# Decay chain and dt-scaled inputs in PSUM banks: a one-layer hybrid attention and state-space kernel

## The chip, the core and the metric

The kernel runs on one core of a Trainium2 chip. The metric is the device time of one execution in microseconds (us). Engines are named as in the profile: PE (TensorE matmul), PEld (its weight load), DVE (VectorE), ACT (ScalarE), POOL (GpSimd) and SP (the queue that issues the loads).

## What is computed

One layer: a projection of the normed input feeds sparse attention and a Mamba-2 state-space mixer; both are merged, and a gated MLP follows. The change lies in the mixer, which works on 4 chunks of 128 tokens and 4 groups of 8 heads:

```python
x = (xh.astype(f32) * dt[..., None]).reshape(b, nc, q, g, r, p)
a_cum = jnp.cumsum(adt, axis=2)
seg = a_cum[:, :, :, None] - a_cum[:, :, None, :]
decay = jnp.exp(jnp.where(tri[None, None, :, :, None, None], seg, -jnp.inf))
cb = jnp.einsum("bclgn,bcsgn->bclsg", cm, bm)
y_diag = jnp.einsum("bclsgr,bcsgrp->bclgrp", cb[..., None] * decay, x)
states = jnp.einsum("bclgn,bclgrp->bcgrpn", bm, x * decay_states[..., None])
```

## The kernel before

All matrices are split into a high and a low part in the matmul format (`hi` on ACT, `lo = src - hi` on DVE or, for weights, on POOL), and three matmuls make one product. Weights come through `weight()`: a 512 KB load on SP, `wh` on ACT (L86), `wl` on POOL (L87).

The mixer runs group by group. `ssd_chain` writes the steps of one group; `weave` spreads matmul work that does not depend on them between the steps: the projections `pxbc` of the next group (convolved on DVE, L388), the gate projections `pz`, and the output projection `pso` of the group before. The top-128 search of the indexer (L332, L333, tile `msk`) is independent DVE work beside groups 0 and 1. A scheduler of the framework then fixes each engine's order and the buffers of each pool, and every engine executes its own order strictly.

Two steps matter here. `prep_M` builds the masked decay matrix of four heads: a load of the cumulative sums as `dec` (128x512), four subtractions (L524), an exponential on ACT (L526), the product with `cb` (L527), and the split into `Mh` (ACT) and `Ml` (DVE). `prep_x` transposes a chunk into the PSUM tile `px`, scales it by dt into the SBUF tile `xdt` (L500), makes `y` (L502), splits `xdt` into `X2` (printed as X) in two halves (L507 ACT, L508 DVE), scales `xdt` once more in place (L513) and splits it into `xwh` and `xwl`. `diag` multiplies `M` by `X2` into `py`. There are 32 `prep_M` and 16 `prep_x`; 12 of these make `xw`.

PSUM has two pools of four banks: `pm` (through `mmt`) for the long projections, `pc` (through `cht`) for everything small: `pcb`, `px`, `py`, `po`, `pst`, `pB`, `pyT`.

Of the kernel before, what the change touches and what calls it, by code (L numbers as in the profile page):

```python
# [9 lines left out]
F32 = mybir.dt.float32  # L10
# [4 lines left out]
P = 128  # L15
# [7 lines left out]
HG = 8  # L23
# [25 lines left out]
def _body(ctx, tc, x, prm_d, cst_d, nfin_d, wI_d, wX_d, wSO_d, wQ_d, wG_d, wAO_d, wO_d, wUp_d, wDn_d,  # L49
# [32 lines left out]
    ident = cv("ident")  # L82

    def split(hi, lo, src, lo_eng=None):
        """hi = fp32r(src), lo = fp32r(src - hi)."""
        nc.scalar.activation(hi, src, AF.Copy)  # L86
        (lo_eng or nc.vector).tensor_tensor(lo, src, f(hi), OP.subtract)  # L87

# [10 lines left out]
        return hi, lo  # L99

    def mm3(ps, terms):
        """ps = sum of lhs.T @ rhs over terms of ((lhs_hi, lhs_lo), (rhs_hi, rhs_lo))."""
        seq = [(a[0], b[0]) for a, b in terms] + [(a[0], b[1]) for a, b in terms] + [(a[1], b[0]) for a, b in terms]
        for i, (l, r) in enumerate(seq):
            nc.tensor.matmul(ps, l, r, start=(i == 0), stop=(i == len(seq) - 1))  # L105

    def rsqrt(dst, ss, scale, eps, n, pool):
        """dst = (ss*scale + eps)^-0.5"""
        t = pool.tile([P, n], F32, tag="rsq", name="rsq")
        nc.vector.tensor_scalar(t, ss, scale, eps, OP.mult, OP.add)  # L110
        nc.gpsimd.tensor_tensor(dst, t, mhalf[:, :n], OP.pow)
# [5 lines left out]
            for k in range(KD)]  # L117

    def norm_T(xts, gname, dst, pool, sq, scl):
        """dst = rmsnorm(xts).T in hi and lo; sq and scl: the engine (ACT or DVE) of each block's squares and scaling."""  # L120
        for hf in range(2):
            alloc = mmt if hf == 0 else cht
            ps = [alloc(f"nT{gname}{hf}{i}").rearrange("p (k n) -> p k n", k=2) for i in range(KD // 2)]
            for bb in range(2):
                b = 2 * hf + bb
                xn = pool.tile([P, D], F32, tag="xn", name=f"xn{gname}{b}", bufs=4)
                ss = pool.tile([P, 1], F32, tag="nss", name=f"nss{gname}{b}", bufs=4)
                rs = pool.tile([P, 1], F32, tag="nrs", name=f"nrs{gname}{b}", bufs=4)
                if sq[b] == "v":
                    nc.vector.scalar_tensor_tensor(xn, xts[b], 1.0, xts[b], OP.mult, OP.mult, accum_out=ss)  # L130
                else:
                    nc.scalar.activation(xn, xts[b], AF.Square, accum_out=ss)
                rsqrt(rs, ss, 1.0 / D, EPS, 1, pool)
                if scl[b] == "a":
                    nc.scalar.activation(xn, xts[b], AF.Copy, scale=rs)
                else:
                    nc.vector.tensor_scalar(xn, xts[b], rs, None, OP.mult)
                for k in range(KD):
                    nc.tensor.transpose(ps[k // 2][:, k % 2, bb * P:(bb + 1) * P], xn[:, k * P:(k + 1) * P], ident)
            hs = slice(hf * 256, (hf + 1) * 256)  # L140
            for k in range(KD):
                g = pv(gname, k, k + 1)
                p_ = ps[k // 2][:, k % 2, :]
                nc.scalar.activation(dst[k][0][:, hs], p_, AF.Copy, scale=g)  # L144
                nc.vector.scalar_tensor_tensor(dst[k][1][:, hs], p_, g, f(dst[k][0][:, hs]), OP.mult, OP.subtract)
# [6 lines left out]
    def proj_T(ps, w):  # L152
        mm3(ps, [((w[0][:, k * P:(k + 1) * P], w[1][:, k * P:(k + 1) * P]), actT[k]) for k in range(KD)])

# [1 line left out]
    mid_stack = ExitStack()  # L156
    mid = mid_stack.enter_context(tc.tile_pool(name="mid", bufs=1, side="right"))
    ckvT = (mid.tile([P, S], R32, tag="ckh", name="ckh"), mid.tile([P, S], R32, tag="ckl", name="ckl"))
# [16 lines left out]
    with tc.tile_pool(name="n1", bufs=2) as n1:  # L175
# [15 lines left out]
        nc.sync.dma_start(cs1, cst_d[:, NKEEP:])  # L191
        norm_T(xts, "gmix", actT, n1, "vava", "aavv")

# [1 line left out]
        ps = mmt("pkidx")  # L195
        psc = mmt("pcr")
        for hf in range(2):
# [33 lines left out]
            nc.scalar.activation(ckvT[0], pk, AF.Copy)  # L231
            nc.vector.tensor_tensor(ckvT[1], pk, f(ckvT[0]), OP.subtract)

# [1 line left out]
        dx = dtS.rearrange("p a b -> p (a b)")  # L235
        e = n1.tile([P, 128], F32, tag="sp_e", name="sp_e", bufs=1)
        z = n1.tile([P, 128], F32, tag="sp_z", name="sp_z", bufs=1)
# [35 lines left out]

        latent()

# [1 line left out]
        pu = cht("pu")  # L277
        nc.tensor.matmul(pu[:H, :UW], pv("relb")[:BUCKETS, :], oh, start=True, stop=True)
        us = n1.tile([H, UW], F32, tag="us", name="us", bufs=1)
        nc.vector.tensor_copy(us, pu[:H, :UW])  # L280
        nc.sync.dma_start(uD, us)

# [1 line left out]
    nc.vector.tensor_copy(msk[:, 0:P], cv("maskc"))  # L284
    sds = ExitStack()
    sd = sds.enter_context(tc.tile_pool(name="sd", bufs=2))

    def dup_q(ps, name, tags, pool, scale, bufs):
        """Per head of a pair, its rows hi and lo on both halves of the partitions."""
        out = []  # L290
        for hh in range(2):
            r, o = slice(64 * hh, 64 * hh + 64), slice(64 - 64 * hh, 128 - 64 * hh)
            hi = pool.tile([P, S], R32, tag=tags[2 * hh], name=f"{name}h{hh}", bufs=bufs)
            lo = pool.tile([P, S], R32, tag=tags[2 * hh + 1], name=f"{name}l{hh}", bufs=bufs)
            nc.scalar.activation(hi[r], ps[r], AF.Copy, scale=scale)
            nc.vector.scalar_tensor_tensor(lo[r], ps[r], scale, f(hi[r]), OP.mult, OP.subtract)
            nc.sync.dma_start(f(hi[o]), f(hi[r]))
            nc.sync.dma_start(f(lo[o]), f(lo[r]))
            out.append((hi, lo))
        return out  # L300
# [37 lines left out]
            out += [lambda r=rnd, k=k: r(k=k) for k in range(16)]  # L338
        return out

# [1 line left out]
    def weave(chain, fill):  # L342
        """Emit the chain's (weight, step)s in order, the fillers spread between them by weight."""
        total = sum(w for w, _ in chain) or 1
        acc = done = 0
        for w, step in chain:
            step()
            acc += w
            want = int(len(fill) * acc / total + 1e-6)
            for k in range(done, want):  # L350
                fill[k]()
            done = want
        for k in range(done, len(fill)):
            fill[k]()

    def proj_steps(name, wsrc, after, parts=2):
        """One column tile of a projection of actT, in emission steps."""
        st = {}

        def seq():  # L360
# [114 lines left out]
    def ssd_chain(g, X, Z, uss):  # L475
# [17 lines left out]
        def prep_x(c):  # L493
# [2 lines left out]
            for j in range(4):  # L496
                nc.tensor.transpose(px[:, j * P:(j + 1) * P], X[j][:, cs], ident)
            px3 = px.rearrange("p (r q) -> p r q", r=HG)
            xdt = sd.tile([P, HG, 64], F32, tag="xdt", name=f"xdt{g}_{c}", bufs=1)
            nc.vector.tensor_tensor(xdt, px3, bc(dtS[:, c, hs], 64), OP.mult)  # L500
            y = sd.tile([P, HG, 64], F32, tag="y", name=f"y{g}_{c}", bufs=4)
            nc.vector.tensor_tensor(y, px3, bc(pv("dsk")[:, hs], 64), OP.mult)  # L502
            st["y"][c] = y
            for half in range(2):
                X2 = sd.tile([P, 4, 2, 64], R32, tag="X2", name=f"X2{g}_{c}_{half}", bufs=4)
                xh = xdt[:, 4 * half:4 * half + 4, :]
                nc.scalar.activation(X2[:, :, 0, :], xh, AF.Copy)  # L507
                nc.vector.tensor_tensor(X2[:, :, 1, :], xh, f(X2[:, :, 0, :]), OP.subtract)  # L508
                st["X2"][c, half] = X2
            if c < NB - 1:  # L510
                xwh = sd.tile([P, S], R32, tag="xwh", name=f"xwh{g}_{c}", bufs=1)
                xwl = sd.tile([P, S], R32, tag="xwl", name=f"xwl{g}_{c}", bufs=1)
                nc.vector.tensor_tensor(xdt, xdt, bc(dst8[:, c, hs], 64), OP.mult)  # L513
                split(xwh, xwl, xdt.rearrange("p r q -> p (r q)"), lo_eng=nc.vector)
                st["xw"][c] = (xwh, xwl)

        def prep_M(c, half):
# [2 lines left out]
            nc.sync.dma_start(dec, bass.AP(tensor=acD.tensor, offset=acD.offset + (c * 32 + r0) * P,  # L520
                                           ap=[[0, P], [1, 4 * P]]))
            cbb = st["cb"][:, c, :].unsqueeze(1).to_broadcast([P, 4, P])
            for r in range(4):
                nc.vector.tensor_scalar(dec[:, r, :], dec[:, r, :], acS[:, c, r0 + r:r0 + r + 1], 0.0,  # L524
                                        OP.subtract, OP.min)
            nc.scalar.activation(dec, dec, AF.Exp)  # L526
            nc.vector.tensor_tensor(dec, dec, cbb, OP.mult)  # L527
            Mh = sd.tile([P, 4, P], R32, tag="Mh", name=f"Mh{g}_{c}_{half}", bufs=3)
            Ml = sd.tile([P, 4, P], R32, tag="Ml", name=f"Ml{g}_{c}_{half}", bufs=3)
            split(Mh, Ml, dec, lo_eng=nc.vector)  # L530
            st["M"][c, half] = (Mh, Ml)

        def diag(c, half):
# [114 lines left out]
    prev[0]()  # L648
    last_trans, so_last = prev[1:]

# [1 line left out]
    attT = []  # L652
    ao_stack = ExitStack()

# [128 lines left out]
    crs = {}  # L783

    def pav_(h):
        """Even heads: [Vh|Vl], odd heads: [Vl|Vh], so that the low part lands on the other half of the partitions."""
        p, hh = h // 2, h % 2
        r, o_ = slice(64 * hh, 64 * hh + 64), slice(64 - 64 * hh, 128 - 64 * hh)
        V, PT = Vs[p // 2], PTs[h]
# [65 lines left out]
        weave(chain, fl)  # L855
    att_split(7)

# [1 line left out]
    at.close()  # L859
    nxs = ExitStack()  # L860
    nx = nxs.enter_context(tc.tile_pool(name="nx", bufs=1, side="right"))
# [15 lines left out]
        split(hi, lo, tg)  # L877
        mg.append((hi, lo))

# [1 line left out]
    x1 = [big.tile([P, D], F32, tag=f"ys{b}", name=f"x1{b}") for b in range(NB)]  # L881
    for b in range(NB):
        nc.sync.dma_start(x1[b], x[b * P:(b + 1) * P, :])
# [120 lines left out]


def _coltile(w):
    """(K, N) -> (N/128, 128, K/128 * 128): per column tile, rows on partitions."""
    k, n = w.shape
    return np.ascontiguousarray(w.reshape(k // P, P, n // P, P).transpose(2, 1, 0, 3)).reshape(n // P, P, k)

# [75 lines left out]
```

## Time and profile before

| | us |
|---|---|
| three runs | 1187.9, 1189.9, 1190.06; median 1189.9 |
| span of the profiled execution | 1188.0 |
| PE busy | 1113.1 (94%) |
| DVE busy | 705.9 (59%) |
| ACT busy | 582.3 (49%) |
| POOL busy | 518.0 (44%) |

The profiled execution is known by its span alone; the median of the runs is 1.9 us above it. An instruction counts as busy from its start to its end, also where it has started and is held up, so a DVE instruction that is far longer than others of its form has been waiting inside its own bar. The mixer takes from about 76 us to 480 us, attention to about 690, merge and output projection to 820, the MLP the rest.

### The profile page before, as it was taken

The page shows a single profiled execution, that of the slowest core. Times are in us where ns is not written, and L with a number is a line of the kernel's source. Part 1 is how long each engine was busy: PE and PEld are TensorE (multiplying, and loading weights), DVE is VectorE, ACT ScalarE, POOL GpSimd, SP SyncE. Part 2 cuts the span into 40 slices and gives each one's busy share as a digit, 9 for nine tenths or more (in the row PEclk, how much of TensorE's full clock was granted, in tenths as well). Part 3 has the DMA queues.
Part 4 walks back from the last instruction along what each step waited for, and adds up shares of the span by engine and source line. Part 5 has one row for each costly group of instructions (what it writes and reads, how often), then busy time and mean ns, then how long its engine had stood idle before and what let it go on. Part 6 is the DMA issues. An engine that isn't in the chain of part 4 may idle for free.

```text
span 1188.0 us, 14616 instructions
## 1 busy us (share of the span) xinstructions
PE 1113.1 (94%) x5268; PEld 920.8 (78%) x5268; DVE 705.9 (59%) x1324; ACT 582.3 (49%) x942; POOL 518.0 (44%) x287
## 2 busy tenths in 40 slices
PE   5898996998999889899999899999999999999997
PEld 5677775876887678778878788888888888888885
DVE  5569999998579689368988833305533344330004
ACT  5356464557476555456667633215444444432113
POOL 3324343334524434566566444444444444444442
PEclk9989999999999899999999999999999999999999
DMA  5264322222322231443434133232332222222221
GB/s 186 90 184 143 107 81 80 89 87 74 116 80 83 86 116 59 122 127 107 129 102 125 47 110 123 107 110 86 106 106 90 104 91 99 97 89 107 89 105 73
DMA packets 43306, 122.06 MB, mean 103 GB/s; under 512 B 5393, under 2 KB 9761, under 8 KB 43233
## 3 DMA queue, kind: packets, MB, share of 16 engines
q1 hardware_dynamic: 42656, 120.07, 30.5%
q8 instruction: 42, 0.69, 0.2%
q10 hardware_dynamic: 576, 1.05, 0.2%
q14 instruction: 32, 0.25, 0.1%
HBM read 108.29 MB, written 5.32 MB: 96 GB/s over the span
## 4 chain that ended last, share of the span: by engine, by line
PE 57%; DVE 26%; ACT 5%; issue 3%; POOL 2%; DMA 2%; POOLq 0%; DVEq 0%; ACTq 0%
PE pup L105 20%; PE pdn L947 10%; PE pso L464 5%; PE pao L105 4%; PE pga L105 4%; PE pwo L891 3%; DVE dec L524 3%; DVE u L388 3%; PE pxbc L373 3%; DVE msk L333 2%; DVE dec L527 2%; DVE m L332 2%; DVE pr L747 1%; DVE pr L759 1%; DVE Ml L87 1%
## 5 line engine op out<-in xcount | busy, mean ns | idle before, releaser
L87 POOL TENSOR_TENSOR wl<-wr,wh 128x1024 fp32r<-128x1024 f32 x168 | 409.8, 2440 | 481.4 <-ACT wh L86 260.6
L86 ACT ACTIVATE wh<-wr 128x1024 fp32r<-128x1024 f32 x168 | 177.4, 1057 | 189.1 <-PE pdn L947 80.6
L930 DVE SCALAR_TENSOR_TENSOR fu<-pup,prm,fu 128x511 f32<-128x511 f32 x88 | 65.9, 749 | 124.2 <-ACT fu L928 122.6
L105 PE MATMUL pup<-hTh,wh 128*128 128x512 f32 (+1 forms) x368 | 88.0, 381 | 1.6 <-ACT hTh L144 0.8
L105 PE MATMUL pup<-hTl,wh 128*128 128x512 f32 (+1 forms) x368 | 87.7, 380 | 0.0
L105 PE MATMUL pup<-hTh,wl 128*128 128x512 f32 (+1 forms) x368 | 87.5, 380 | 0.0
L105 PEld LDWEIGHTS pup<-hTh,wh 128*128 128x128 f32 x368 | 67.2, 188 | 15.1 <-ACT hTh L144 1.1
L105 PEld LDWEIGHTS pup<-hTl,wh 128*128 128x128 f32 x368 | 67.2, 188 | 13.1
L105 PEld LDWEIGHTS pup<-hTh,wl 128*128 128x128 f32 x368 | 67.2, 188 | 13.1
L947 PE MATMUL pdn<-wl,fh 128*128 128x512 f32 x176 | 68.6, 390 | 1.2 <-POOL wl L87 1.2
L947 PE MATMUL pdn<-wh,fl 128*128 128x512 f32 x176 | 68.5, 389 | 0.0
L947 PE MATMUL pdn<-wh,fh 128*128 128x512 f32 x176 | 68.4, 390 | 0.0
L974 DVE TENSOR_TENSOR x<-pdn,x 128x512 f32<-128x512 f32 x8 | 5.5, 690 | 104.6 <-PE pdn L947 104.6
L439 PE MATMUL pz<-wh,hTh 128*128 128x512 f32 x128 | 52.4, 409 | 9.9 <-DVE u L388 9.9
L388 DVE SCALAR_TENSOR_TENSOR u<-pxbc,prm,u 128x511 f32<-128x511 f32 (+2 forms) x72 | 53.2, 739 | 9.7 <-ACT u L386 9.3
L373 PE MATMUL pxbc<-hTh,wh 128*128 128x512 f32 x192 | 53.8, 413 | 4.1 <-ACT wh L86 2.9
L524 DVE TENSOR_SCALAR dec<-dec,acS 128x128 f32<-128x128 f32 x128 | 50.6, 450 | 8.9 <-DMA dec<-acD 8.9
L373 PE MATMUL pxbc<-hTh,wl 128*128 128x512 f32 x192 | 51.1, 393 | 0.0
L440 PE MATMUL pz<-wl,hTh 128*128 128x512 f32 x128 | 50.9, 398 | 0.0
L441 PE MATMUL pz<-wh,hTl 128*128 128x512 f32 x128 | 50.9, 398 | 0.0
L373 PE MATMUL pxbc<-hTl,wh 128*128 128x512 f32 x192 | 50.0, 391 | 0.0
L464 PE MATMUL pso<-yTh,wh 128*128 128x512 f32 x128 | 38.7, 426 | 11.4 <-ACT wh L86 7.9
(360 smaller groups left out, 2554.2 us busy)
## 6 DMA issues: line engine op xcount, KB each, us to landing
wr<-wUp SPq DMA_DIRECT2D x44, 512.0 KB, 3.4
wr<-wX SPq DMA_DIRECT2D x40, 512.0 KB, 3.5
wr<-wDn SPq DMA_DIRECT2D x22, 512.0 KB, 3.5
dec<-acD SPq DMA_DIRECT2D x32, 256.0 KB, 3.3
wr<-wSO SPq DMA_DIRECT2D x16, 512.0 KB, 3.5
wr<-wG SPq DMA_DIRECT2D x16, 512.0 KB, 3.6
x<-x SPq DMA_DIRECT2D x8, 512.0 KB, 4.9
wr<-wQ SPq DMA_DIRECT2D x8, 512.0 KB, 3.5
```

Source lines behind the costliest of these rows:

```text
L86: nc.scalar.activation(hi, src, AF.Copy)
L87: (lo_eng or nc.vector).tensor_tensor(lo, src, f(hi), OP.subtract)
L105: nc.tensor.matmul(ps, l, r, start=(i == 0), stop=(i == len(seq) - 1))
L373: nc.tensor.matmul(st["ps"], *st["it"][i], start=(i == 0), stop=(i == 23))
L388: nc.vector.scalar_tensor_tensor(u[:, d:], ps[:, :S - d], pv("cw", o + 3 - d, o + 4 - d), u[:, d:], OP.mult, OP.add)
L439: nc.tensor.matmul(ps, actT[k][0][:, bs], wh[:, ws], start=(k == 0), stop=False)
L440: nc.tensor.matmul(ps, actT[k][0][:, bs], wl[:, ws], start=False, stop=False)
L441: nc.tensor.matmul(ps, actT[k][1][:, bs], wh[:, ws], start=False, stop=(k == KD - 1))
L464: nc.tensor.matmul(ps, *seq[i], start=(i == 0), stop=(i == 11))
L524: nc.vector.tensor_scalar(dec[:, r, :], dec[:, r, :], acS[:, c, r0 + r:r0 + r + 1], 0.0, OP.subtract, OP.min)
L930: nc.vector.scalar_tensor_tensor(u[:, d:], ps[:, :S - d], pv("fw", o + 2 - d, o + 3 - d), u[:, d:], OP.mult, OP.add)
L947: nc.tensor.matmul(po8[b][hf], l[:, bs], r[:, ws], start=(k == 0 and i == 0), stop=(k == NF - 1 and i == 2))
```

## The change

`prep_M` writes the result of the four subtractions into a PSUM tile `pd` of the pool `pc` and runs the exponential, the product with `cb` and the split there; `dec` is only the landing place of the load. `prep_x` makes `y` first, then scales `px` by dt in place in PSUM, and both splits read `px`; `xdt` is gone (its buffer stays in use for `t1` in `off`). The number of instructions on DVE, ACT and PE in these steps stays the same. Comments and docstrings are dropped too.

```diff
-            xdt = sd.tile([P, HG, 64], F32, tag="xdt", name=f"xdt{g}_{c}", bufs=1)
-            nc.vector.tensor_tensor(xdt, px3, bc(dtS[:, c, hs], 64), OP.mult)
             y = sd.tile([P, HG, 64], F32, tag="y", name=f"y{g}_{c}", bufs=4)
             nc.vector.tensor_tensor(y, px3, bc(pv("dsk")[:, hs], 64), OP.mult)
             st["y"][c] = y
+            nc.vector.tensor_tensor(px3, px3, bc(dtS[:, c, hs], 64), OP.mult)
             for half in range(2):
                 X2 = sd.tile([P, 4, 2, 64], R32, tag="X2", name=f"X2{g}_{c}_{half}", bufs=4)
-                xh = xdt[:, 4 * half:4 * half + 4, :]
+                xh = px3[:, 4 * half:4 * half + 4, :]
...
-                nc.vector.tensor_tensor(xdt, xdt, bc(dst8[:, c, hs], 64), OP.mult)
-                split(xwh, xwl, xdt.rearrange("p r q -> p (r q)"), lo_eng=nc.vector)
+                nc.vector.tensor_tensor(px3, px3, bc(dst8[:, c, hs], 64), OP.mult)
+                split(xwh, xwl, px)
...
+            pd = cht(f"pd{g}_{c}_{half}").rearrange("p (r q) -> p r q", r=4)
             for r in range(4):
-                nc.vector.tensor_scalar(dec[:, r, :], dec[:, r, :], acS[:, c, r0 + r:r0 + r + 1], 0.0,
+                nc.vector.tensor_scalar(pd[:, r, :], dec[:, r, :], acS[:, c, r0 + r:r0 + r + 1], 0.0,
                                         OP.subtract, OP.min)
-            nc.scalar.activation(dec, dec, AF.Exp)
-            nc.vector.tensor_tensor(dec, dec, cbb, OP.mult)
+            nc.scalar.activation(pd, pd, AF.Exp)
+            nc.vector.tensor_tensor(pd, pd, cbb, OP.mult)
...
-            split(Mh, Ml, dec, lo_eng=nc.vector)
+            split(Mh, Ml, pd)
```

The scheduler's order changes with it. On DVE, in group 0 while the top-128 search runs, the kernel before emits the subtractions of a tile in a block, well ahead of `cb` (the number behind a tile is the buffer's; x4 stands for four rows alike):

```order
L388 SCALAR_TENSOR_TENSOR u_871<-pxbc_837,prm,u_871 128x510
L524 TENSOR_SCALAR dec_1_0_1132<-dec_1_0_1132,acS 128x128
L388 SCALAR_TENSOR_TENSOR u_871<-pxbc_837,prm,u_871 128x509
L524 TENSOR_SCALAR dec_1_0_1132<-dec_1_0_1132,acS 128x128 x3
L524 TENSOR_SCALAR dec_1_1_1217<-dec_1_1_1217,acS 128x128 x4
L332 MAX m_1_1717<-msk 128x8
```

In the changed kernel the first subtractions come just ahead of `cb`; the brackets say what an instruction waits for:

```order
L524 TENSOR_SCALAR pd_0_0_1078<-dec_0_0_1076,acS 128x128 [waits DMAHW6_49]
L333 MATCH_REPLACE msk<-m_1_1721,msk 128x256 [waits DVE_49]
L524 TENSOR_SCALAR pd_0_0_1078<-dec_0_0_1076,acS 128x128 [waits DVE_49]
L332 MAX m_1_1721<-msk 128x8 [waits DVE_49]
L524 TENSOR_SCALAR pd_0_0_1078<-dec_0_0_1076,acS 128x128 [waits DVE_49]
L333 MATCH_REPLACE msk<-m_1_1721,msk 128x256 [waits DVE_49]
L524 TENSOR_SCALAR pd_0_0_1078<-dec_0_0_1076,acS 128x128 [waits DVE_49]
L332 MAX m_1_1721<-msk 128x8 [waits DVE_49]
L333 MATCH_REPLACE msk<-m_2_1722,msk 128x384
L489 TENSOR_TENSOR cb_1056<-pcb_1043,cst 128x512 [waits PE_49]
```

The subtractions have moved behind a large part of the search, each waits for the one before it into the same tile, and most of the time another instruction stands between: 83 of the 128 wait for DVE's own earlier work (7 before), and 8 of these stand directly behind their predecessor.

On ACT, the first `prep_x` of group 0 reads before, with both halves of `X2` one behind the other:

```order
L86 ACTIVATE Mh_0_0_1084<-dec_0_0_1076 128x512 [waits DVE_49]
L86 ACTIVATE Mh_0_1_1128<-dec_0_1_1120 128x512 [waits DVE_49]
L86 ACTIVATE Mh_1_0_1140<-dec_1_0_1132 128x512 [waits DVE_49]
L507 ACTIVATE X_0_0_1097<-xdt_0_1093 128x4x64 [waits DVE_49]
L507 ACTIVATE X_0_1_1100<-xdt_0_1093 128x4x64
L86 ACTIVATE wh_1267<-wr_1265 128x1024 [waits DMAHW6_49,PE_49,Pool_49]
L86 ACTIVATE xwh_0_1103<-xdt_0_1093 128x512 [waits DVE_49]
```

And in the changed kernel:

```order
L526 ACT_TABLE_LOAD
L526 ACTIVATE pd_0_0_1078<-pd_0_0_1078 128x512 [waits DVE_49]
L86 ACTIVATE Mh_0_0_1085<-pd_0_0_1078 128x512 [waits DVE_49]
L506 ACTIVATE X_0_0_1097<-px_0_1089 128x4x64 [waits DVE_49,PE_49]
L86 ACTIVATE wh_1269<-wr_1267 128x1024 [waits DMAHW6_49,PE_49,Pool_49]
L506 ACTIVATE X_0_1_1100<-px_0_1089 128x4x64 [waits DVE_49]
L526 ACTIVATE pd_0_1_1122<-pd_0_1_1122 128x512 [waits DVE_49]
L526 ACTIVATE pd_1_0_1135<-pd_1_0_1135 128x512 [waits DVE_49]
```

The second half of `X2` now waits for DVE in all 16 `prep_x` (in none before), since the two engines take turns on one bank, and the exponentials stand one or a few at a time: the order holds 42 table loads on ACT, against 38.

## Rows read from the trace of the kernel before

**Rows 1.** Windows of the mixer: length, then busy us of PE, PEld, DVE, ACT, POOL, PE clock.

```profile
76.00:236.00 160.00, 142.74 (x677) 116.84 (x676) 155.33 (x336) 89.42 (x132) 60.27 (x27) 0.97 0.33 108
236.00:480.00 244.00, 228.68 (x1097) 188.13 (x1096) 196.22 (x340) 146.76 (x221) 97.95 (x48) 0.96 0.25 87
```

**Rows 2.** The chain that ended last, mixer alone (76:480), shares by line.

```profile
by line: PE pso L464 10.7%; DVE dec L524 8.9%; DVE u L388 8.2%; PE pxbc L373 7.5%; DVE msk L333 6.2%; DVE dec L527 5.5%; DVE m L332 5.0%; DVE Ml L87 4.0%; DVE X L508 3.6%; issue 3.2%; DMA dec<-acD 2.5%; DVE xwl L87 1.8%; DVE Hl L87 1.7%; DV
```

**Rows 3.** Waits of PE in 76:480: total us, times, longest.

```profile
PE pz L439 <- DVE u L388: 9.9, 3, 6.4
PE pso L464 <- ACT wh L86: 4.9, 2, 4.2
```

**Rows 4.** DVE groups in 76:480: count, busy us, mean ns, idle before.

```profile
L524 DVE TENSOR_SCALAR dec<-dec,acS 128x128 f32<-128x128 f32 x128 | 50.6, 450 | 8.9 <-DMA dec<-acD 8.9
L527 DVE TENSOR_TENSOR dec<-dec,cb 128x512 f32<-128x512 f32 x32 | 27.5, 880 | 5.6 <-ACT dec L526 5.6
L87 DVE TENSOR_TENSOR Ml<-dec,Mh 128x512 fp32r<-128x512 f32 x32 | 25.8, 807 | 2.8 <-ACT Mh L86 2.7
L508 DVE TENSOR_TENSOR X<-xdt,X 128x256 fp32r<-128x256 f32 x32 | 20.5, 674 | 0.0
L87 DVE TENSOR_TENSOR xwl<-xdt,xwh 128x512 fp32r<-128x512 f32 x12 | 10.0, 836 | 0.1
```

**Rows 5.** Single lines on DVE: duration in ns, least, median, most.

```profile
L524 DVE TENSOR_SCALAR dec<-dec,acS x128: 262/277/2501, 98.8 to 444.9; 128x128 f32<-128x128 f32 x128
L527 DVE TENSOR_TENSOR dec<-dec,cb x32: 669/681/2337, 128.1 to 447.9; 128x512 f32<-128x512 f32 x32
L87 DVE TENSOR_TENSOR Ml<-dec,Mh x32: 670/682/2728, 129.9 to 466.1; 128x512 fp32r<-128x512 f32 x32
L508 DVE TENSOR_TENSOR X<-xdt,X x32: 401/416/2614, 131.7 to 470.0; 128x256 fp32r<-128x256 f32 x32
L87 DVE TENSOR_TENSOR xwl<-xdt,xwh x12: 675/679/2546, 134.5 to 461.6; 128x512 fp32r<-128x512 f32 x12
L502 DVE TENSOR_TENSOR y<-px,prm x16: 666/678/692, 131.1 to 468.5; 128x512 f32<-128x512 f32 x16
```

**Rows 6.** Timeline of DVE and POOL, 241.8:250: start us, us, instruction.

```profile
242.48 3.43 DVE L508 TENSOR_TENSOR X<-xdt,X 128x256 fp32r<-128x256 f32 x2
...
248.75 0.40 DVE L541 TENSOR_TENSOR y<-y,py 128x256 f32<-128x256 f32 x1
249.08 0.73 DVE L388 SCALAR_TENSOR_TENSOR u<-pxbc,prm,u 128x509 f32<-128x509 f32 x1
...
243.05 2.58 POOL L87 TENSOR_TENSOR wl<-wr,wh 128x1024 fp32r<-128x1024 f32 x1
```

**Rows 7.** POOL group in 76:480.

```profile
L87 POOL TENSOR_TENSOR wl<-wr,wh 128x1024 fp32r<-128x1024 f32 x52 | 129.5, 2492 | 168.1 <-ACT wh L86 132.9 <-PE pxbc L373 11.7 <-PE pqidx L105 11.2
```

**Rows 8.** The chain in 230:240, a piece: start us, us, what.

```profile
235.79 1.37 DVE dec L524 x7
```

**Rows 9.** Timeline of DVE, 272.3:274.0, an instruction that waits for the one before.

```profile
272.94 0.41 DVE L541 TENSOR_TENSOR y<-y,py 128x256 f32<-128x256 f32 x1
273.39 0.42 DVE L542 TENSOR_TENSOR y<-y,py 128x256 f32<-128x256 f32 x1
```

**Rows 10.** Timeline of DVE, 130.4:137.2, the first `prep_x`.

```profile
130.49 0.68 DVE L500 TENSOR_TENSOR xdt<-px,dtS 128x512 f32<-128x512 f32 x1
131.09 0.68 DVE L502 TENSOR_TENSOR y<-px,prm 128x512 f32<-128x512 f32 x1
...
134.49 2.55 DVE L87 TENSOR_TENSOR xwl<-xdt,xwh 128x512 fp32r<-128x512 f32 x1
```

**Rows 11.** ACT groups in 76:480.

```profile
L526 ACT ACT_TABLE_LOAD x17 | 21.8, 1283 | 7.3 <-DVE dec L524 5.6 <-issue 1.4
L86 ACT ACTIVATE Mh<-dec 128x512 fp32r<-128x512 f32 x32 | 19.9, 624 | 23.1 <-DVE dec L527 23.1
```

**Rows 12.** What SP's queue waited for, whole span.

```profile
SPq L520 <- DVE Ml L87: 86.4, 24, 11.2
```

## Prediction

> **What bounds the kernel now.** Read first where the mixer loses time. PE is the engine to keep busy; in the two windows of the mixer [rows 1] it is busy 142.7 of 160.0 us and 228.7 of 244.0 us, so it idles 32.6 us in 404. From 76 to 236 us DVE is busy 155.3 of 160.0 us: it is the bound there. From 236 us on it is busy 196.2 of 244.0 us and PE is ahead of it. The chain that ended last, read for the mixer alone [rows 2], agrees: its largest shares beside the matmuls are DVE lines, and the five of them that the change touches (L524 8.9%, L527 5.5%, Ml 4.0%, X 3.6%, xwl 1.8%) make 23.8% of 404 us, 96 us. The waits of PE [rows 3] lead back to DVE too: the longest is a projection `pz` whose bank the convolution L388 on DVE has not yet emptied (9.9 us in 3 waits), and a weight part `wh` that ACT makes late (4.9 us) is late because ACT stands behind DVE results in its own order.
>
> Then read why DVE is so busy. The groups [rows 4] show means far above the medians of the same lines [rows 5]: L524 takes 277 ns in the median, 450 in the mean and 2501 at worst. The timeline shows what the long ones are [rows 6]: two L508, 0.42 us each by their median, hold DVE for 3.43 us, and they end at 245.91 us, just after POOL's `wl` ends at 243.05 + 2.58 = 245.63. So a DVE instruction that takes all its tensors from SBUF can be shut out for as long as POOL works, and POOL does 52 such splits of 2.49 us in the mixer [rows 7], with its other work 158 of 404 us [rows 1]. The row of L502, which reads the PSUM tile `px`, has 666 to 692 ns in all 16 [rows 5]: no such wait. An instruction with a PSUM operand and at most one SBUF tensor is what all touched DVE lines become.
>
> **The change part by part.** *Waits taken away.* Mean minus median, times the count, from [rows 4, 5]: L524 128 x (450 - 277) = 22.1 us, L508 32 x (674 - 416) = 8.3, L527 32 x (880 - 681) = 6.4, Ml 32 x (807 - 682) = 4.0, xwl 12 x (836 - 679) = 1.9; together 42.7 us of DVE. Not all of it is won: POOL's work stays, and the next instruction on DVE with all its tensors in SBUF (Hl, the gate product `zs`, Bl, Cl, some of `msk`: about 45, where 236 touched ones fall away) will meet it. At the mean of 42.7 / 236 = 0.18 us for each they bear 8 us as before; at twice that, 8 us more. I take the 8 off: 35 us. The lower bound is 20 us, if half of the waits only land elsewhere.
>
> *The subtraction L524 itself.* No row shows DVE writing PSUM. Seven in a row take 1.37 us [rows 8], 0.196 us from start to start. Below: nothing more, since L502 with its PSUM input costs the same 678 ns as L527 does from SBUF (681) [rows 5]. Above: the 416 ns of a 256-wide instruction [rows 5], 139 ns more, 128 x 0.139 = 18 us. Between them stands L388, which also reads PSUM and a per-partition scalar: 0.73 us at 509 elements [rows 6]; with (681 - 416) / 256 = 1.04 ns for each element [rows 5], 128 elements of it make 0.73 - 381 x 0.00104 = 0.33 us, against 0.277. I take this: 128 x 0.056 = 7 us.
>
> [...]
>
> *Waits added on DVE.* In the order, 76 more subtractions wait for their predecessor into the same tile, but only 8 stand directly behind it. What that costs shows at L541 and L542: 0.45 us from start to start [rows 9], against 0.33 where no such wait is [rows 6]; 0.12 us. So 8 x 0.12 = 1 us, at most 76 x 0.12 = 9.
>
> *Handover on ACT.* The second half of X2 waits for DVE in 16 places, and behind it on ACT stand `wh` splits and exponentials, for which POOL and then PE wait. Four more table loads of 1.283 us [rows 11] are 5 us of ACT. ACT is busy 236 of 404 us [rows 1], so I price both at nothing directly; without that cover they cost 5 us and 16 x 0.4 us, 11 in all. Against this stand ACT's present waits for L527 (23.1 us before Mh) [rows 11], which shrink with the lock waits.
>
> *PSUM banks.* `px` is held from the first read to `xwl`: 130.49 to 137.04 us in the first `prep_x` where it was free after 131.77 [rows 10], 5.3 us more, 16 times, 85 us of bank time. `pd` is held for at least 4 x 0.2 + 0.6 + 0.7 + 0.6 + 0.7 = 3.4 us, by the handovers perhaps 10: 32 of them make 109 to 320 us. Four banks offer 4 x 404 = 1616 us; 12 to 25% more of that is used. PE's own stretch behind a late bank would be `px`, `py`, `po`, `pst` and all the projections queued after it. I take 4 us on PE for this and the ACT handovers together; the lower bound is nothing.
>
> *Loads.* `dec` is free after the fourth subtraction, no longer after Ml. SP stood 86.4 us at these loads for Ml, the weight loads behind it [rows 12], and DVE 8.9 us for late `dec` [rows 4]; the chain holds 2.5% of 404 us, 10 us, of `dec` landing [rows 2]. I take 3 us, since each load can now be issued earlier and its subtraction stands later, while DVE has other work in part of that time; bounds 0 and 9.
>
> *The sum.* The touched lines have 50.6 + 27.5 + 25.8 + 20.5 + 10.0 = 134 us of busy time [rows 4], of which 96 us, 72%, lie on the chain [rows 2]. So of DVE's net 35 - 7 - 1 = 27 us some 19 reach the end. With 3 for the loads and minus 4 for banks and handovers: 18 us, about half of PE's idle 32.6, which is the most that can be had from this side. 1188.0 - 18 = 1170 us for the profiled execution; with the 1.9 us by which the runs' median lies above it, **1172 us**. Its own range goes from 20 us of relief (12 net, 9 on the chain, 8 us in all) to a subtraction that costs no more than now and no late bank (34 x 0.72 + 3 = 27 us): 1163 to 1182.
>
> **The rivals.**
> *PE starves for banks (slower).* The small tiles of PE take some 96 banks of `pc` in the mixer (per group pcb, 4 px, 8 py, 3 po, 3 pst, pB, 4 pyT), now 32 `pd` rotate with them, and PE takes its order strictly: one late bank stops the projections behind it. The gain of 18 us is eaten at 0.19 us of waiting for each of the 96; at 0.35 us the time is 34 us worse than forecast without it, 1206 us, at 0.25 us 1196. For it: a bank now hangs on ACT and DVE in turn, and DVE remains about 80% busy. Against it: the bank time above, a quarter more at most, and the two longest waits of PE now are for a bank of `pm` and for a weight [rows 3], not for `pc`. Chance 0.19.
> *The relief ends nowhere (no change).* From 236 us on PE is busy 94%; if the waits removed were slack there, and the first window only trades the search for the decay chain, DVE's 27 us pass into its own idle time: 1188 to 1192 us. Against it: 72% of these lines lie on the chain. Chance 0.11.
> *PSUM dearer than taken (small gain).* With both upper bounds, 18 us for L524 and 9 us for the waits on its own work, the net of DVE is 35 - 27 = 8 us, 6 on the chain, 5 us in all: 1185 us. For it: no row shows DVE writing PSUM. Against it: L502 and L527 take the same [rows 5]. Chance 0.09. [...]
> *More than forecast.* [...] Chance 0.08.
>
> **How the numbers follow.** The forecast itself has 0.53. Faster by over 0.2% (2.4 us, about what a measurement of this kernel can tell from no change) adds the small gain and the large one: 0.70; same 0.11; slower 0.19. The range reaches below to the large gain and above into the starved case, 1157 to 1196, which leaves out some 0.13, most of it above.
>
> **What would show it.** In the changed profile L524 should lie at 0.28 to 0.34 us with hardly any above 1 us, and the means of L527, Ml, X and xwl at their medians; DVE busy in the mixer about 325 us where it had 352; long DVE bars only on Hl, `zs`, Bl and Cl. PE's idle time in the mixer should fall to some 15 us, and no `px` or `py` should wait for a bank of `pc`. The prediction is wrong if these waits appear, if L524 writes PSUM at 0.4 us or more, or if the mixer's end moves while attention behind it gives the time back.

## The result and the profile after

The changed kernel takes 1160.88 us in the median of four runs (1160.16 to 1162.26), the kernel before, run beside it, 1189.23 us (1187.9 to 1190.06): 28.4 us less, a ratio of 0.9765 with a 95% interval of 0.9746 to 0.9783. All of it is won in the mixer. From the first matmul of the attention to the end of the program both take the same, 709 and 710 us. The windows of the mixer, cut from the first `pxbc` to the first matmul of the attention, are the measure used from here on: length, then busy us of PE, PEld, DVE, ACT and POOL, then PE's granted clock. First the kernel before:

```profile
76.10:478.80 402.70, 370.12 (x1765) 303.93 (x1764) 350.69 (x674) 235.97 (x352) 158.22 (x75) 0.96 0.28 96
```

And the changed kernel, with the two windows that answer to [rows 1] ahead of it (the second ends 30 us earlier now):

```profile
76.00:236.00 160.00, 151.10 (x714) 124.29 (x713) 149.89 (x346) 98.15 (x143) 61.66 (x29) 0.97 0.34 110
236.00:450.00 214.00, 211.02 (x1056) 175.20 (x1055) 175.80 (x330) 143.15 (x215) 92.14 (x46) 1.00 0.30 97
...
75.22:448.81 373.59, 361.71 (x1765) 299.18 (x1764) 324.57 (x673) 240.69 (x356) 154.17 (x75) 0.99 0.32 103
```

The mixer is 29.1 us shorter. DVE is busy 26.1 us less. PE's idle time falls from 402.70 - 370.12 = 32.6 us to 11.9, and its 1765 matmuls take 8.4 us less, with the granted clock at 0.99 where it was 0.96: 20.7 + 8.4 = 29.1. After 236 us PE idles 3 us in 214.

The groups of DVE in 76:456, which answer to [rows 4] (count, busy us, mean ns, idle time before):

```profile
L524 DVE TENSOR_SCALAR pd<-dec,acS 128x128 f32<-128x128 f32 x128 | 42.6, 346 | 0.7
L527 DVE TENSOR_TENSOR pd<-pd,cb 128x512 f32<-128x512 f32 x32 | 22.1, 694 | 6.2 <-ACT pd L526 5.8
L87 DVE TENSOR_TENSOR Ml<-pd,Mh 128x512 fp32r<-128x512 f32 x32 | 21.9, 685 | 6.9 <-ACT Mh L86 6.6
L572 DVE TENSOR_TENSOR zs<-y,zs 128x512 f32<-128x512 f32 x16 | 18.6, 1163 | 0.1
...
L87 DVE TENSOR_TENSOR Hl<-Hs,Hh 128x512 fp32r<-128x512 f32 x12 | 14.3, 1195 | 0.5 <-ACT Hh L86 0.4
L507 DVE TENSOR_TENSOR X<-px,X 128x256 fp32r<-128x256 f32 x32 | 13.3, 416 | 2.0 <-ACT X L506 2.0
```

And single lines, which answer to [rows 5] (least, median, most in ns):

```profile
L524 DVE TENSOR_SCALAR pd<-dec,acS x128: 329/346/357, 120.3 to 441.5; 128x128 f32<-128x128 f32 x128
...
L527 DVE TENSOR_TENSOR pd<-pd,cb x32: 674/696/700, 124.8 to 442.6; 128x512 f32<-128x512 f32 x32
...
L87 DVE TENSOR_TENSOR Ml<-pd,Mh x32: 671/684/693, 126.3 to 444.0; 128x512 fp32r<-128x512 f32 x32
...
L87 DVE TENSOR_TENSOR xwl<-px,xwh x12: 673/686/692, 135.2 to 432.3; 128x512 fp32r<-128x512 f32 x12
L87 DVE TENSOR_TENSOR Hl<-Hs,Hh x12: 674/689/2176, 139.9 to 437.1; 128x512 fp32r<-128x512 f32 x12
...
L507 DVE TENSOR_TENSOR X<-px,X x32: 404/415/425, 130.0 to 443.2; 128x256 fp32r<-128x256 f32 x32
```

On every touched line the longest instruction now lies within 4% of the median; before, each had one above 2300 ns [rows 5]. The long bars that are left stand mostly on `Hl` and `zs`, which still take both their tensors from SBUF: their means are 1195 and 1163 ns, and `Hl` has one of 2176.

The chain that ended last, for 76:456, by line (to be held against [rows 2]):

```profile
by line: PE pxbc L373 15.6%; PE pso L464 12.9%; PE pz L441 3.2%; PE pz L439 3.1%; PE pz L440 3.1%; PE py L538 2.2%; DVE pd L524 1.6%; PE py L539 1.5%; DVE pd L527 1.4%; PE pst L105 1.4%; DVE Ml L87 1.3%; ACT zs L602 1.2%; issue 1.1%; DVE zs
```

The five touched lines held 23.8% of it; what is left of them in this row is L524 1.6, L527 1.4 and Ml 1.3%, and `dec` landing is gone from it. The chain now runs through the matmuls.

### The profile page after: what moved, and what is told of

It is laid out like the page before. It is cut to its first block, busy times and chain, and to the rows that moved or that the text cites. A ratio compares the mean times of both kernels' runs of the same rounds, so it can differ in the third digit from the quotient of the medians.

```text
span 1158.8 us, 14580 instructions
## 1 busy us (share of the span) xinstructions
PE 1104.0 (95%) x5268; PEld 914.1 (79%) x5268; DVE 681.3 (59%) x1324; ACT 586.0 (51%) x946; POOL 514.0 (44%) x287
## 3 DMA queue, kind: packets, MB, share of 16 engines
q1 hardware_dynamic: 42656, 120.07, 32.6%
## 4 chain that ended last, share of the span: by engine, by line
PE 61%; DVE 10%; ACT 4%; issue 3%; POOL 3%; DMA 1%; POOLq 0%; DVEq 0%; ACTq 0%
PE pup L105 21%; PE pdn L947 10%; PE pso L464 6%; PE pxbc L373 5%; PE pao L105 4%; PE pga L105 4%; PE pwo L891 3%; DVE pr L747 2%; DVE pr L759 1%; ACT pr L754 1%; PE pz L441 1%; PE pz L439 1%; PE pz L440 1%; POOL wl L87 1%; POOL bm L731 1%
## 5 line engine op out<-in xcount | busy, mean ns | idle before, releaser
L373 PE MATMUL pxbc<-hTh,wh 128*128 128x512 f32 x192 | 50.9, 397 | 0.0
L928 ACT ACTIVATE fu<-pup,prm 128x512 f32<-128x512 f32 x44 | 34.3, 780 | 27.2 <-PE pup L105 27.2
L754 ACT ACTIVATE pr<-pr,mx 128x128 f32<-128x128 f32 (+1 forms) x64 | 35.5, 556 | 15.6 <-DVE mx L751 15.6
```

The costliest lines, as they stand in the source:

```text
L373: nc.tensor.matmul(st["ps"], *st["it"][i], start=(i == 0), stop=(i == 23))
L754: nc.scalar.activation(pr[:, o:o + n], pr[:, o:o + n], AF.Exp, bias=mx[:, i:i + 1], accum_out=sm[:, i:i + 1])
```

## The experiments

The theory: DVE is shut out by POOL when it takes all its tensors from SBUF, and the change wins by giving such instructions a PSUM operand. Rivals: the gain comes from `dec` being free after the subtractions (earlier loads); or from some other part of the new order. In the table, "lock waits" is worked out from the bars of DVE in the mixer: of each bar that is over 150 ns longer than the lower quartile of its line and form, the excess, summed. (The median will not do, since of `Bl`, for one, two bars in four are long.)

The two traces bear out the first half of the theory and narrow it. In the mixer of the kernel before there are 43 such bars. Each starts while an instruction of POOL runs and ends 0.08 to 0.56 us after that one ends; 33 of them stand behind a `wl` split, 10 behind other work of POOL (`Hs` and `y`). But not every instruction with its tensors in SBUF is held. Of 21 instructions with two tensors from SBUF that start while a split has over 0.9 us left to run, 17 take 1518 to 2904 ns and four 679 to 682; the four start in two splits that themselves take 3.5 us, where the median of the 52 is 2.4. Of the top-128 search (L332, L333, one large tensor) 17 start in this way, and none takes more than 687 ns, its usual time; all 9 subtractions that start so take 1300 ns or more. In the changed kernel 35 subtractions start so, and none takes more than 357 ns.

Mixer and DVE busy are rows of the windows, each from the profiled execution. That execution was 3.9 us above the median for "decay alone, L524 in SBUF", 2.9 for "before, POOL in halves", 2.1 for "changed, L524 in SBUF", and within 1.2 us of it elsewhere. The kernel before had medians of 1189.2 to 1191.0 us beside the kernels of the table; where a difference is small, go by the ratio.

| kernel | us | ratio to before, 95% interval | mixer | DVE busy | lock waits |
|---|---|---|---|---|---|
| before | 1189.2 | 1 | 402.7 | 350.7 | 56.4 |
| changed | 1160.9 | 0.9765 (0.9746 to 0.9783) | 373.6 | 324.6 | 19.3 |
| decay chain alone | 1170.9 | 0.9836 (0.9805 to 0.9867) | 383.3 | 337.2 | 33.3 |
| dt-scaled inputs alone | 1199.3 | 1.0079 (1.0052 to 1.0105) | 413.2 | 349.0 | 55.0 |
| the latter, X2 whole | 1197.7 | 1.0065 (1.0047 to 1.0083) | 409.6 | 350.2 | 57.0 |
| before, `dec` freed early | 1196.7 | 1.0045 (1.0027 to 1.0063) | 410.1 | 352.3 | 57.5 |
| changed, L524 in SBUF | 1162.8 | 0.9773 (0.9747 to 0.98) | 377.6 | 331.5 | 34.4 |
| decay alone, L524 in SBUF | 1171.6 | 0.9838 (0.9809 to 0.9867) | 387.5 | 344.1 | 49.0 |
| before, POOL in halves | 1184.5 | 0.9942 (0.9924 to 0.996) | 399.3 | 346.1 | 49.7 |
| changed, POOL in halves | 1154.2 | 0.9699 (0.9673 to 0.9724) | 368.5 | 314.5 | 8.7 |
| changed, POOL in quarters | 1151.9 | 0.9661 (0.9632 to 0.9689) | 367.5 | 312.5 | 5.7 |
| quarters, X2 whole | 1150.8 | 0.9669 (0.9642 to 0.9697) | 367.3 | 310.6 | 6.8 |
| before, no `wl` in mixer | 1154.1 | 0.9696 (0.9676 to 0.9716) | 366.7 | 299.1 | 4.7 |
| changed, no `wl` in mixer | 1147.2 | 0.9637 (0.9613 to 0.966) | 361.4 | 306.0 | 1.8 |

**The parts alone.** Decay chain only (`dec` to `pd` in `prep_M`; `prep_x` as before):

```diff
-                nc.vector.tensor_scalar(dec[:, r, :], dec[:, r, :], acS[:, c, r0 + r:r0 + r + 1], 0.0,
+                nc.vector.tensor_scalar(pd[:, r, :], dec[:, r, :], acS[:, c, r0 + r:r0 + r + 1], 0.0,
...
-            split(Mh, Ml, dec, lo_eng=nc.vector)
+            split(Mh, Ml, pd)
```

> Only the decay chain moves to PSUM; the dt-scaled inputs stay in the SBUF tile xdt. Theory of the lock (DVE instructions with all tensors in SBUF wait for POOL's weight splits, and taking those waits away is the gain): the lines moved carried 22.1 + 6.4 + 4.0 = 32.5 of the 42.7 us of such waits, so about 21 of the 28.4 us come: 1166 to 1171 us, L524 near 346 ns with no long ones, X and xwl still with long ones. Rival (the gain is the early release of the landing tile dec and the new order): the release is all in this half, so 1160 to 1164 us.

The scaled inputs only (`xdt` to `px` in `prep_x`; `prep_M` as before):

```diff
-                xh = xdt[:, 4 * half:4 * half + 4, :]
+                xh = px3[:, 4 * half:4 * half + 4, :]
...
-                split(xwh, xwl, xdt.rearrange("p r q -> p (r q)"), lo_eng=nc.vector)
+                split(xwh, xwl, px)
```

> Only the dt-scaled inputs move to PSUM; the decay chain stays in dec. Theory of the lock: X and xwl carried 8.3 + 1.9 = 10.2 of 42.7 us of waits, so about 7 us: 1180 to 1185 us; the waits of L524 stay or grow. Rival (release of dec): nothing, 1188 to 1191 us.

The decay chain alone brings 18.5 us, within the range of the lock theory. The scaled inputs alone cost 10 us, which lies outside both ranges, and yet on top of the decay chain they bring 10 (1170.9 to 1160.9): the parts do not add. The DVE groups of the mixer with the scaled inputs alone show why nothing is won:

```profile
L523 DVE TENSOR_SCALAR dec<-dec,acS 128x128 f32<-128x128 f32 x128 | 54.3, 476 | 13.0 <-DMA dec<-acD 13.0
...
L526 DVE TENSOR_TENSOR dec<-dec,cb 128x512 f32<-128x512 f32 x32 | 28.5, 907 | 1.6 <-ACT dec L525 1.4
L87 DVE TENSOR_TENSOR Ml<-dec,Mh 128x512 fp32r<-128x512 f32 x32 | 28.1, 883 | 2.5 <-ACT Mh L86 2.5
L507 DVE TENSOR_TENSOR X<-px,X 128x256 fp32r<-128x256 f32 x32 | 13.2, 414 | 3.9 <-ACT X L506 3.8
```

X has lost its waits (mean 414 ns against 674), but the next SBUF instructions meet POOL instead: L523, L526 and Ml have risen from 450, 880 and 807 ns [rows 4] to 476, 907 and 883, and the lock waits as a whole have hardly fallen (55.0 us against 56.4). `dec`, which those lines hold, lands late more often (13.0 us of waiting against 8.9). That makes no gain, not yet a loss; so the handover was tried by itself, with X2 made by one ACT and one DVE instruction per chunk, so that the bank changes hands once:

```diff
+            X2 = sd.tile([P, HG, 2, 64], R32, tag="X2", name=f"X2{g}_{c}", bufs=2)
+            nc.scalar.activation(X2[:, :, 0, :], px3, AF.Copy)
+            nc.vector.tensor_tensor(X2[:, :, 1, :], px3, f(X2[:, :, 0, :]), OP.subtract)
```

> The kernel with only the dt-scaled inputs in PSUM (1199.3 us, 10 us slower than before), with X2 made by one ACT instruction and one DVE instruction for a whole chunk, so that the two engines take the bank of px over from each other once instead of twice. If the alternation of the halves on one bank is what made it slower: back to 1188 to 1192 us. If it is that the waits for POOL only land on the decay lines (their total was 55 us, 53 before) and that px holds its bank longer: 1195 to 1200 us.

1197.7 us: the handover theory falls. Its DVE group shows the subtractions with the same burden and more waiting for the load:

```profile
L522 DVE TENSOR_SCALAR dec<-dec,acS 128x128 f32<-128x128 f32 x128 | 54.1, 473 | 17.1 <-DMA dec<-acD 17.1
```

In these two kernels DVE's busy time is no longer than before (349.0 and 350.2 us against 350.7); its idle time is, 64.2 and 59.4 us against 52.0. Later landings make 4 and 8 us of that (13.0 and 17.1 against 8.9). PE, too, now waits with `pyT`, which does not read `xwl`, for the bank that `px` holds until `xwl` is made: 3.1 us with the scaled inputs alone and 1.9 with X2 whole, where the kernel before has no such wait:

```profile
PE pyT L607 <- DVE xwl L87: 3.1, 1, 3.1
```

Whether these two make the whole loss, and why the loads land later, was not separated. In the other half, the decay chain alone, PE waits for banks of `pc` as well:

```profile
PE po L105 <- DVE Ml L87: 4.4, 1, 4.4
PE px L497 <- DVE Ml L87: 2.0, 3, 1.3
```

Neither `po` nor `px` reads `Ml`; they wait for the bank of a `pd`. With 3.4 us for three other banks that `px` waits for, this is 9.8 us, where the changed kernel has 3.2. So 6.6 of the 10 us that the scaled inputs bring on top lie here; that `px` in PSUM is the reason was not tested.

**When `dec` is freed.** The kernel before, with the subtractions written into the SBUF tile of `Ml`, where the exponential and the product then work; no PSUM:

```diff
+            pd = Ml
             for r in range(4):
-                nc.vector.tensor_scalar(dec[:, r, :], dec[:, r, :], acS[:, c, r0 + r:r0 + r + 1], 0.0,
+                nc.vector.tensor_scalar(pd[:, r, :], dec[:, r, :], acS[:, c, r0 + r:r0 + r + 1], 0.0,
...
```

> The kernel before, with the decay chain worked in the SBUF tile that becomes Ml (the decay matrix is rounded to the matmul format at each step there), so that the landing tile dec is free after the four subtractions while every DVE operand stays in SBUF. Theory of the lock: the waits for POOL stay as they are, 1184 to 1191 us. Rival (early release of dec and the order it allows): most of the change's gain is here, 1163 to 1175 us, DVE's wait for a landing dec gone.

It came out 0.45% slower, at 1196.7 us outside both ranges. DVE no longer waits for `dec` to land, as in the changed kernel, so early release alone does not make the gain. But the run says less than it should of its worth: the tile of `Ml`, of which there are three, is now held from the subtraction on, and the order changed too. DVE waits 12.9 us for the exponential, 5.6 before; ACT's groups show 24 table loads at it, where 17 stood [rows 11],

```profile
L529 ACT ACT_TABLE_LOAD x24 | 30.8, 1283 | 19.9 <-DVE Ml L527 19.6
```

and the lock waits, 57.5 us, are no lower than before.

**The subtraction in PSUM or SBUF.** The changed kernel, with L524 left in SBUF and the exponential writing `pd`:

```diff
-                nc.vector.tensor_scalar(pd[:, r, :], dec[:, r, :], acS[:, c, r0 + r:r0 + r + 1], 0.0,
+                nc.vector.tensor_scalar(dec[:, r, :], dec[:, r, :], acS[:, c, r0 + r:r0 + r + 1], 0.0,
...
-            nc.scalar.activation(pd, pd, AF.Exp)
+            nc.scalar.activation(pd, dec, AF.Exp)
```

> The changed kernel, but the four subtractions write back to the SBUF tile dec as before and only the exponential writes into PSUM; dec is free after the exponential. Theory of the lock: L524 is back at 277 ns in the median with some 20 us of long ones in all, against 128 x 69 ns = 9 us that its PSUM form costs; net loss 10 to 13 us of DVE, of which most reach the end: 1166 to 1174 us. Rival (early release of dec and order): the release stays, so 1159 to 1163 us.

And the same with `xdt` in SBUF as well, so beside the decay chain alone:

> Subtractions in the SBUF tile dec, exponential, product and split of the decay chain in PSUM, dt-scaled inputs in SBUF as before. Theory of the lock with the waits counted one by one: only L527 and Ml, 10.4 of 42.7 us, are taken away, 7 us: 1180 to 1185 us. Rival (which of the waits count depends on what stands behind them: those of L524 are slack, those between exponential and diag are not): near the kernel with the whole decay chain in PSUM, 1168 to 1176 us.

1162.8 against 1160.9 us, and 1171.6 against 1170.9: where the subtraction writes is worth 2 and 1 us in the medians, and the intervals overlap. Both times the rival's range held and the lock theory's did not. Counted one by one, the waits are not worth their length: the subtraction carries 22 of the 42.7 us, and in the second run 49.0 of 56.4 us of lock waits are still there, yet 19 us are won. The kernel before with POOL in halves (below) has as many lock waits, 49.7 us, and takes 1184.5 us. What differs most between these two is DVE's idle time, 43.4 and 53.2 us, and 7.5 us of that is the wait for `dec`, which is free after the exponential in the first (10.2 us in the other):

```profile
DVE dec L525 <- DMA dec<-acD: 2.7, 2, 1.5
```

So the earlier release counts here. It was not told apart from the rival's own reason, that a wait costs by what stands behind it. In the first of the two runs, the single line shows both sides of the trade, 275 ns in the median and waits up to 2443:

```profile
L524 DVE TENSOR_SCALAR dec<-dec,acS x128: 258/275/2443, 97.7 to 417.1; 128x128 f32<-128x128 f32 x128
```

Its waits (24.8 us) relieve `zs` and `Hl` of most of theirs (13.7 to 5.4 us), and each of 128 instructions is cheaper; what remains is 7 us more of DVE and 4 us of mixer, half of which is the execution's distance from its median.

**POOL taken away.** In both kernels the low part of the mixer's weights is left out and the matmuls read the high part in its place, so that of POOL's 52 splits there two are left, for the attention behind it, and PE has as many matmuls as ever:

```diff
+        if mixer[0]:
+            nc.scalar.activation(hi, raw, AF.Copy)
+            return hi, hi
```

> The kernel before, with the low part of the mixer's weights left out: POOL does no weight splits from the first pxbc to the last group, and the matmuls read the high part in its place, so their number and shape stay. Theory of the lock: nearly all 53 us of long DVE bars in the mixer go, L524, L527, X, Ml come down to their medians without any PSUM, and the kernel gains at least what the change gained: 1152 to 1164 us. Rival (early release, order, PSUM itself): the splits are off the path, the time stays within 5 us: 1184 to 1191 us.

> The changed kernel with the same low part of the mixer's weights left out. Theory of the lock: only the 19 us of waits left in it can go, 3 to 8 us faster: 1152 to 1158 us, and against the kernel before with the same left out the change gains nothing or costs up to 5 us, since L524 pays 69 ns more each and nothing is won. Rival (early release, order, PSUM itself): the gap to the kernel before with the same left out stays near 28 us.

The windows of the mixer, kernel before without the splits:

```profile
70.66:437.37 366.71, 358.69 (x1765) 299.30 (x1764) 299.06 (x670) 235.57 (x352) 33.24 (x25) 0.99 0.33 104
```

And the changed kernel without them:

```profile
72.61:433.98 361.37, 355.76 (x1766) 295.65 (x1765) 306.01 (x673) 240.74 (x356) 33.73 (x25) 1.00 0.33 107
```

The kernel before, with every tile still in SBUF, loses 35 us by this alone, more than the change brings: its DVE is busy 51.6 us less, which is what its lock waits fall by (56.4 to 4.7), and PE idles 8.0 us where it idled 32.6. So POOL's splits are what DVE was waiting for. One side effect was not separated: a weight's landing buffer is free earlier, after ACT's `wh`. PE never waits for POOL's `wl` in the mixer before, and for ACT's `wh` 7.8 us there and 1.7 here, so some 6 of the 35 us may come that way. The pair misses the second forecast of the lock theory: the change still brings 7 us when hardly a split is left to wait for, although DVE is then busy 7 us more; what falls is DVE's idle time, 67.7 to 55.4 us. One wait is nearly as large as that, in the kernel before without splits:

```profile
DVE dec L528 <- DMA dec<-acD: 11.1, 10, 3.3
```

In the changed kernel without splits there is none. So of the 28.4 us some 7 come without the splits, by the earlier loads and the new order less what PSUM costs DVE, and some 21 hang on the splits, if the two add; that they do was not shown, and the parts above did not.

**POOL's instruction made shorter.** The weight split in two, then in four instructions of 256 columns, first on the kernel before:

```diff
-        split(hi, lo, raw, lo_eng=nc.gpsimd)
+        nc.scalar.activation(hi, raw, AF.Copy)
+        for a in range(0, w, 256):
+            nc.gpsimd.tensor_tensor(lo[:, a:a + 256], raw[:, a:a + 256], f(hi)[:, a:a + 256], OP.subtract)
```

> The kernel before with each weight's POOL split cut into two instructions of 512 columns; nothing else. Theory of the lock: every wait of DVE is at most half as long and some 20 to 25 of the 48 us of long bars in the mixer go: 1172 to 1182 us. Rival (release and order): 1186 to 1192 us.

> The changed kernel with each weight's POOL split cut into two instructions of 512 columns, so that one instruction shuts DVE out half as long. Theory of the lock: the 19 us of waits left (Hl, zs, Bl, some msk) halve in length but may double in number; POOL gets a little longer by its fixed cost; between 3 us faster and 2 us slower than the changed kernel, 1158 to 1163 us, and no DVE bar of those lines above some 2.0 us. Rival (DVE no longer matters at all, PE is the bound): the same time as the changed kernel within 1 us.

> The changed kernel with each weight's POOL split cut into four instructions of 256 columns. The waits left on DVE (8.9 us with halves) halve again, while POOL pays its fixed cost of some 0.25 us twice more for each weight: 1151 to 1156 us, between 3 us faster and 2 us slower than with halves. If the projections after the mixer come to wait for wl the time rises above 1156 us.

> The changed kernel with POOL's weight split in quarters of 256 columns (1151.9 us) and, besides, X2 made whole by one ACT and one DVE instruction per chunk: 16 instructions fewer on each engine and no second handover of the bank. If the handover or the fixed cost of an instruction still reaches the end: 2 to 5 us below, 1147 to 1150 us. If the handover is free, as ACT's waits in the changed kernel say (1.0 us): the same within 2 us, 1150 to 1154 us, or worse by the longer time until the first diag can start.

On the kernel before, halves bring 0.6% (1184.5 us beside 1191.0, between the two forecasts) and leave 49.7 of 56.4 us of waits: they are shorter but more (27 on L524 where there were 16), as if a DVE instruction that one half no longer shuts out met the next, or its neighbour did. On the changed kernel, with few candidates left, halves take the waits from 19.3 to 8.7 us and the time to 1154.2, below the forecast, quarters to 5.7 us and 1151.9, although POOL is then busy longer: its group with quarters, in the mixer, is

```profile
L100 POOL TENSOR_TENSOR wl<-wr,wh 128x256 fp32r<-128x256 f32 x208 | 153.1, 767 | 157.8 <-ACT wh L98 105.8 <-PE pxbc L375 15.7 <-issue 11.3
```

against 52 x 2492 ns, 129.5 us [rows 7]. POOL has the room. The version with quarters beats both kernels: 39 us below the kernel before that ran beside it (1191.0), 9 below the changed one (12 by the ratios); X2 made whole besides changes nothing that can be told (1150.8 us in another comparison, ratios 0.9661 and 0.9669). So no cost of the second handover of `px`'s bank shows here; a small one could be hidden, since the first `diag` starts later with X2 whole.

## Why the prediction was right, and where it was short

The direction held, and the mechanism in the main; the size, 18 us, was 10 short, and the time fell outside the forecast's own range, below its 1163 us, where the rival "more than forecast" stood. The range on record, 1157 to 1196 us, holds it only because it reached down to that rival, which had a chance of 0.08; as far as the size goes, that was luck.

- **Waits taken away: right as a sum.** All 42.7 us of them are gone from the touched lines. 8 us more were to land elsewhere; by the count of the table the untouched lines bore 13.6 us and now bear 19.3, 5.7 more. `zs` has risen from 12.6 to 18.6 us and `Hl` from 10.4 to 14.3, while `Bl` and `msk` fell; in the kernel before the two were

```profile
L572 DVE TENSOR_TENSOR zs<-y,zs 128x512 f32<-128x512 f32 x16 | 12.6, 785 | 0.2
...
L87 DVE TENSOR_TENSOR Hl<-Hs,Hh 128x512 fp32r<-128x512 f32 x12 | 10.4, 868 | 0.3 <-ACT Hh L86 0.2
```

  What the prediction had too wide is "all its tensors from SBUF": the search was never held. In the changed kernel L527 with one SBUF input never exceeds 700 ns, `Hl` with two still reaches 2176, and the search with one was not held. The subtraction within SBUF has one too and was held; what sets it apart from the search, no run shows.
- **L524 in PSUM: right.** 0.056 us each was taken. The bar has grown by 69 ns (277 to 346), and what counts, from start to start, by 57. DVE's timeline of the changed kernel has four that do not wait for one another and four that do:

```profile
130.32 1.10 DVE L524 TENSOR_SCALAR pd<-dec,acS 128x128 f32<-128x128 f32 x4
...
388.32 1.52 DVE L524 TENSOR_SCALAR pd<-dec,acS 128x128 f32<-128x128 f32 x4
```

  (1.10 - 0.346) / 3 = 0.251 us, against 0.196 in [rows 8]; (1.52 - 0.346) / 3 = 0.391 where each waits for the one before. 20 pairs in the mixer do the latter, where 8 were counted in the order: 20 x 0.14 = 2.8 us where 1 was forecast. The 57 ns make 7 us. L527, Ml, X and xwl, which now read PSUM, have medians 1 ns shorter to 15 ns longer than before.
- **DVE's net: right.** 26.1 us less of DVE where 27 was forecast, 325 us busy as foretold.
- **The conversion: too low, the step that failed.** "72%, lie on the chain ... some 19 reach the end" took the chain's shares for a rate of exchange. DVE's 26.1 us less of work and 3 us less of idle time (52.0 to 49.0) are the mixer's 29.1: nothing of what DVE saved went into idle time, where the 72% had some 8 us going. The share on the chain before says where the chain went, not what PE would do with an earlier input. The cap of 32.6 us of idle time, "the most that can be had from this side", left out that PE's own busy time can fall: 8.4 of the 29.1 us, at a granted clock of 0.99 for 0.96, which the forecast did not count. All of it is no rate either: with L524 in SBUF 6.9 us more of DVE cost 1.9 us, and in the decay chain alone with L524 in SBUF 6.6 us less went with 19 us. How the missing 10 us divide between this term and the loads stays open.
- **Loads: too low.** 3 us was taken of bounds 0 and 9. The wait for `dec` to land went from 8.9 us to none, and in the pair without splits, where the loads are the largest part, the change brings 7. SP's queue still waits at these loads, but now for the subtraction, and less than the 86.4 us of [rows 12]:

```profile
SPq L519 <- DVE pd L524: 62.7, 17, 7.1
```

- **Banks and handovers: about right.** 4 us was taken off, and the slower rival rested on them. (The 85 us of bank time for `px` counted 16 `prep_x`; 12 of them make `xwl`.) Three of PE's waits are for a bank of `pc`, a `po`, a `pyT` and a `px`, none of which reads what it waits for:

```profile
PE pz L439 <- DVE u L388: 3.3, 2, 2.4
...
PE po L105 <- DVE Ml L87: 1.8, 1, 1.8
...
PE pyT L608 <- DVE yTl L613: 1.0, 1, 1.0
...
PE px L497 <- DVE Ml L87: 0.4, 1, 0.4
```

  That is 3.2 us, none of it in the kernel before; 2.2 are for the bank of a `pd`. The sign that no `px` should wait for a bank was crossed once, by 0.4 us. The convolution's bank of `pm`, 9.9 us [rows 3], costs 3.3. ACT waits for the handover between the halves of X2 1.0 us in all 16 `prep_x`:

```profile
ACT X L506 <- DVE X L507: 1.0, 2, 0.5
```

  The four more table loads (42 in the order) go with 4.7 us more of ACT in the mixer; PE no longer waits for a `wh`, so no cost of them shows, as priced.
- **The rivals.** PE did not starve for banks, though in the decay chain alone it waited 9.8 us for them; the relief did not end nowhere; PSUM was not dearer than taken. "More than forecast", put at 0.08, came about: 20.7 of PE's 32.6 us of gaps closed, and its granted clock rose from 0.96 to 0.99.

## What to carry to other kernels

Look for DVE lines whose mean lies far above their median while POOL works, as that of L524 did (450 ns against 277). Here such lines were being shut out, and the time was had back by giving one operand a PSUM tile (lock waits from 56.4 to 19.3 us), then by cutting POOL's instruction into shorter ones (to 5.7). Do it for the candidates as a set, since here a wait taken from some of them landed on the next: half of this change was worth minus 10 us alone and plus 10 behind the other half, and POOL's split in halves took away 7 of 56 us of waits before the change and 11 of 19 behind it. When the relieved engine feeds an idle TensorE, do not take its share of the chain for a rate of exchange: the whole change won all that DVE saved, while its parts won anything from 10 us less than nothing to nearly three times what DVE saved.

## What the runs showed of the hardware

- A long DVE bar ends with POOL's work: all 43 in the mixer before start while an instruction of POOL runs and end 0.08 to 0.56 us after it. Among those that start with over 0.9 us of a split left, 17 of the 21 that take two tensors from SBUF were held (1518 to 2904 ns), and all 9 subtractions within SBUF (1300 to 2501); the search's 17, with one large tensor, were not (at most 687).
- A DVE subtraction of 128x128 from SBUF to PSUM starts every 0.253 us where the one within SBUF starts every 0.196 (medians of the pairs in the mixer); two-tensor instructions over 512 columns cost nearly the same from either (681 and 696 ns for L527, 682 and 684 for Ml).
- A wait on DVE's own last instruction adds 0.135 us (0.388 from start to start against 0.253, medians of 20 and 19 pairs).
- POOL's split of 1024 columns costs 2492 ns, of 256 columns 767 ns: four make 3068, 23% more, and the kernel is the faster for it (1151.9 us, 1160.9 with whole splits).
- ACT and DVE taking turns on one PSUM bank show no cost that the runs can tell: 1151.9 and 1150.8 us with two turns per chunk and with one.
